# HGRN2 in a hybrid encoder: the 8-token base products of both heads of a pair in one run of half-array passes

## The chip, the cores and the metric

The kernel runs on one core of one Trainium2 chip. A core has five engines that work side by side, each through its own list of instructions in order: PE (TensorE, matrix products), DVE (VectorE, elementwise), ACT (ScalarE, elementwise and copies), POOL (GpSimd, elementwise) and SP (SyncE, which issues DMAs). An instruction waits, on its own engine, until the instructions it depends on have signalled. Products go to PSUM, a memory of eight banks of 128 x 512 fp32; everything else lives in SBUF. The metric is the device time of one execution in microseconds (us).

## The reference

A two-layer encoder on 512 tokens with 1024 channels, in fp32. Each layer feeds the same x through one input projection into three branches (HGRN2, a dilated sliding-window attention, a latent attention), gates and merges them, projects and normalizes. What the change touches is the HGRN2 branch, a gated linear recurrence run in both directions over 8 heads:

```python
def _gla_scan(q, k, v, log_f):
    '''S_t = diag(f_t) S_{t-1} + k_t v_t^T ; o_t = S_t^T q_t, chunkwise.'''
    ...
    def step(state, inp):
        qi, ki, vi, fi = inp
        b = jnp.cumsum(fi, axis=2)
        o_inter = jnp.einsum('bhtk,bhkv->bhtv', qi * jnp.exp(b), state)
        diff = b[:, :, :, None, :] - b[:, :, None, :, :]
        decay = jnp.where(causal, jnp.exp(jnp.where(causal, diff, 0.0)), 0.0)
        attn = jnp.einsum('bhtk,bhsk,bhtsk->bhts', qi, ki, decay)
        o = o_inter + jnp.einsum('bhts,bhsv->bhtv', attn, vi)
        ...
o_f = _gla_scan(q, k_f, v, lf_f)
o_b = flip(_gla_scan(flip(q), flip(k_b), flip(v), flip(lf_b)))
return (o_f + o_b).reshape(B, S, HG_HEADS * HG_DV)
```

## The kernel before, in words

**Layout.** Channels lie on the 128 partitions, the 512 tokens along the free dimension. An input projection of 128 channels (L300) is 24 PE passes of 128x128 weights against 512 tokens: three products of high and low parts of x and of the weights (`xh`, `xl`; `w_...h`, `w_...l`), eight passes each. The high part of a weight block is made by ACT (L274) and the low part by DVE or POOL (L275).

**HGRN2.** The eight heads are worked in four pairs. For a pair, `hgrn_gates` (L300, L677 to L689) projects `hq`, `hf` (two directions) for each head, 144 passes, and L689 clamps the forget gates `fr`. `hgrn_levels` then works up a tree: at level m = 1, 2, 4, 8, 16, 32, 64 blocks of m tokens are joined to blocks of 2m. Each level multiplies gates into queries (`qq`, L774), into keys (`kk`, L775) and gates into each other (`fr` or `f`, L778), all on DVE. The first product, `qq = q * fr`, is POOL's (L696).

- At m = 4 the **base products** are made: the scores inside blocks of 8 tokens, both directions. DVE takes the reciprocal of the gates (L706); the operands `hk` and `hq` are made half by ACT copies (L714) and half by POOL multiplications (L716), four each a head; sixteen products 64 rows wide go into a bank `hs` (L726, 32 records of 128x64 in the trace, since an fp32 product has two). ACT copies the bank to `hc` (L730), POOL cuts it to triangles `ha` and `hz` (L735), DVE adds them (L739).
- At m = 8 to 64 ACT copies the keys into `kc` (L745), sixteen **level products** a head follow (L757, bank `hs_8`, `hs_16` and so on), and DVE writes them into `ha` under a mask (L767). Only then may `qq` be multiplied on (L774), and only then can the products of the next level start.
- Then come key transposes `hkt` (L790) with their ACT copies (L792), state products `hst` (L801), the state chain `hS` on DVE (L810 to L818), and for the pair the outputs `ho` (L840).

Products 64 rows wide use half of PE's array; they are written as runs, between which PE does projections of the next pair.

**What joins a run.** `hgrn_levels` is a generator. A driver runs the two heads' generators in step; where they yield a list of instructions and a function, it calls both functions one after the other and lets the first product wait for both lists, so that both heads' products stand in one run. The level products and the states are yielded so. The base products are not: each head emits its own, with its own wait.

**What sets the order.** The engines' lists are not written by hand. A scheduler at build time places every recorded instruction by a cost model of its own and by program order, so a change in one place can reorder all engines around it. While a pair is in its tree, PE gets the passes of the next pair's gates and, for pairs 1 and 2, of `dv` (96 passes a block, L319), in pair 4 those of `dl`, `hgg` and others.

Of the kernel before, what the change touches and what calls it, by code (L numbers as in the profile page):

```python
# [45 lines left out]
HALVES = [(slice(64 * i, 64 * i + 64), slice(c + 64 * i, c + 64 * i + 64)) for c in range(0, S, 128) for i in range(2)]  # L46
# [144 lines left out]
def fap(ap, off, dims):  # L191

    return bass.AP(ap.tensor, ap.offset + off, [list(ap.ap[0])] + [list(d) for d in dims])
# [7 lines left out]
def tile_encoder(ctx: ExitStack, tc: tile.TileContext, x, xt, positions, blocks, wuq, wuh, par_in, brow, lbp,  # L201
                 ln_g, ln_b, consts, masks, out):
    nc = tc.nc
# [16 lines left out]
    def t2(name, dt=F32, tag="a2"):  # L220
        return t2p.tile([128, 512], dt, tag=tag, bufs=BUFS[tag], name=name)
# [7 lines left out]
    def at_bank(name):  # L229
        return ps_at.tile([128, 512], F32, tag="at", name=name)  # L230
# [4 lines left out]
    def after(first, *before):  # L235

        for b in before:
            tc.add_manual_dep(first.ins, b.ins.name, mybir.DependencyInfo(
                mybir.DependencyClass.Sync, mybir.DependencyReason.DATA), reason="together")
# [221 lines left out]
    def layer(l, x_src, need_next):  # L461
# [230 lines left out]
        def hgrn_levels(h, g, v):  # L692
# [4 lines left out]
            f2 = t2(f"f2{h}_{l}")  # L697
# [4 lines left out]
            while m < 128:  # L702
                if m == 4:
# [4 lines left out]
                    kds, qds, made = [], [], []  # L708
                    for d in range(2):
# [9 lines left out]
                                fap(rc, R * (1 - d) + scaled // m, [[2, R // 2], [0, m]]), ALU.mult))  # L719
                        kds.append(kd)  # L720
                        qds.append(qd)
                    sc, c = at_bank(f"hs{h}_{l}"), t2(f"hc{h}_{l}")
                    first = None
                    for d in range(2):
                        for n, (rows, at) in enumerate(HALVES):
                            mat = nc.tensor.matmul(sc[rows, 256 * d + 64 * (n // 2):256 * d + 64 * (n // 2) + 64],  # L726
                                                   kds[d][:, at], qds[d][:, at], start=True, stop=True)
                            first = first or mat
                    after(first, *made)
                    A.copy(c, sc)  # L730

                    for d, dst in ((0, a), (1, z)):
# [7 lines left out]
                elif m > 4:  # L740

                    if m < 64:
                        sc = at_bank(f"hs{h}_{m}_{l}")
                    kc = t2(f"kc{h}_{m}_{l}")
                    made = A.copy(fap(kc, 0, [[2 * m, R // 2], [m, 2], [1, m]]),  # L745
                                  fap(kk, 0, [[2 * m, R // 2], [S + m, 2], [1, m]]))
# [15 lines left out]
                    if m != 32:  # L762
                        n = [m in ms for ms in HG_MASKS].index(True)
                        for cols in [slice(0, 128)] if m == 64 else [slice(0, 64), slice(64, 128)]:
                            rows, wd = slice(0, 128) if m == 64 else cols, cols.stop - cols.start
# [21 lines left out]
            for d, blocks in ((0, (0, 1, 2)), (1, (1, 2, 3))):  # L787
# [4 lines left out]
                made = A.copy(kt_[:, :384], tr[:, :384])  # L792
# [23 lines left out]
            for j in (1, 0):  # L816
                c = 192 + 64 * j
# [48 lines left out]
        def dil_qk(hp):  # L866
            t = []
            for g in range(3):
                both = t4(f"dl{g}{hp}_{l}")
                for c0, sc_ in ((C_DQ[g], con[:, O_QS + 4 * g + hp:O_QS + 4 * g + hp + 1]), (C_DK[g], None)):  # L870
                    c = c0 + 128 * hp
                    ps = in_fm(c, f"dl{c}")
                    r = both[:, len(t) % 2]
                    o_ap, i_ap = r, ps
                    if g:
                        o_ap = r.rearrange("p (r i) -> p i r", r=4)
                        i_ap = ps.rearrange("p (i r) -> p i r", r=4)
                    if sc_ is None:
                        A.activation(o_ap, i_ap, AF.Identity, bias=pb(c))
                    else:  # L880
                        last = V.tensor_scalar(o_ap, i_ap, pb(c), sc_, ALU.add, ALU.mult)  # L881
                    t.append(r)
            return t, last
# [231 lines left out]
        for hp in range(4):  # L1115
            both = [hgrn_levels(h, G.pop(h), hv) for h in (2 * hp, 2 * hp + 1)]
            while True:
                parts = [next(g) for g in both]
                if parts[0] is None:
                    continue  # L1120
                if len(parts[0]) > 2:
                    break

                firsts = [go() for _, go in parts]
                after(firsts[0], *parts[0][0], *parts[1][0])
            os_.append(hgrn_pair(hp, parts, hv))
            if hp < 3:
                for h in (2 * hp + 2, 2 * hp + 3):
                    G[h] = hgrn_gates(h)
            if hp < 2:  # L1130
                vs.append(in_tm(C_DV[hp], f"dv{hp}", residues=hp > 0))
        hg = [silu_tile(C_HG + 128 * i, f"hgg{i}", False) for i in range(4)]
        qk, _ = dil_qk(0)
# [167 lines left out]
```

## Time and profile before

| | |
|---|---|
| median of three runs | 1773.09 us (1772.72 to 1774.57) |
| the profiled execution | 1771.63 us |
| its span, first to last instruction | 1769.9 us |
| PE busy | 1741.8 us, 98% of the span |
| DVE busy | 1064.2 us, 60% |
| ACT busy | 730.3 us, 41% |
| POOL busy | 573.8 us, 32% |
| mean granted PE clock | 0.996 of full speed |
| PE idle for DVE's `qq` (L774) ahead of level products | 4.3 us in 6 waits |
| base products | 8 heads in each of 2 layers, 32 records each |

A row of the timeline gives the start in us, the duration, the engine, the line, the operation, the tile written and the tiles read, the shape, how many instructions the row stands for, and in brackets the idle time before it with what ended it. The timeline leaves out the idle time of PE when two runs merely follow each other with a seam. PE's busy time counts a record at half clock as busy for twice as long, so "98% busy" holds slow stretches too; the windows' PEclk shows them.

### The profile page before, as it was taken

The numbers are of one execution on the slowest core, as the hardware profiler recorded it, in microseconds if no ns is written. First come the engines' busy times: TensorE is split into PE (matmuls) and PEld (weight loads), VectorE is DVE, ScalarE is ACT, GpSimd is POOL, SyncE is SP. The second block draws the span as 40 slices with busy tenths as digits, with TensorE's granted clock in tenths as the row PEclk, the third lists the DMA queues.
The fourth block names the chain that finished last, engine by engine and source line by source line (L and its number), as shares of the span: only waits on it lengthen the run. The fifth ranks groups of instructions, "written<-read, shape, count | busy, mean of one in ns | idle before, by whom it ended". The sixth has DMA issues, their size and how long they took to land. (4 is left out here: it accounts for less than half of the span.)

```text
span 1769.9 us, 26458 instructions
## 1 busy us (share of the span) xinstructions
PE 1741.8 (98%) x10616; PEld 1450.5 (82%) x10616; DVE 1064.2 (60%) x1912; ACT 730.3 (41%) x1273; POOL 573.8 (32%) x338
## 2 busy tenths in 40 slices
PE   9999999999999999999999999999999999999997
PEld 7778978988888888887888888888888888888876
DVE  8888777443232566756777778775333324666576
ACT  6445454242424353433254455442424254444330
POOL 0412244233333233333213212532433332433341
PEclk9999999999999999999999999999999999999999
DMA  5223222223222222332332222222223221324221
GB/s 194 84 66 102 73 73 89 73 72 96 79 77 84 70 75 79 113 111 72 119 114 90 84 78 74 89 78 78 72 72 98 82 83 48 99 67 151 72 86 69
DMA packets 77146, 154.15 MB, mean 87 GB/s; under 512 B 37728, under 2 KB 37856, under 8 KB 77024
## 3 DMA queue, kind: packets, MB, share of 16 engines
q1 hardware_dynamic: 77024, 152.47, 27.9%
q8 instruction: 83, 1.36, 0.3%
q14 instruction: 39, 0.32, 0.1%
HBM read 148.15 MB, written 4.29 MB: 86 GB/s over the span
## 5 line engine op out<-in xcount | busy, mean ns | idle before, releaser
L775 DVE TENSOR_TENSOR kk<-kk,fr 128x512 f32<-128x512 f32 x96 | 94.0, 999 | 30.0 <-ACT kc L745 18.9
L696 POOL TENSOR_TENSOR qq<-hq,fr 128x1024 f32<-128x1024 f32 x16 | 42.5, 2654 | 201.6 <-DVE fr L689 181.9
L774 DVE TENSOR_TENSOR qq<-qq,fr 128x512 f32<-128x512 f32 x96 | 75.3, 797 | 16.9 <-POOL qq L696 15.2
L1079 DVE TENSOR_SCALAR mg<-mg 128x512 f32<-128x512 f32 x32 | 53.2, 1669 | 49.0 <-ACT mg L1078 48.9
L898 DVE CUSTOM_DVE_ANT_0 zb<-dsb,con 128x256 f32<-128x256 f32 x64 | 23.3, 421 | 46.4 <-PE dsb L951 46.3
L767 DVE COPY_PREDICATED ha<-mask,hs 64x256 f32<-64x256 uint8 (+1 forms) x80 | 40.4, 505 | 16.7 <-PE hs L757 15.6
L275 POOL TENSOR_TENSOR wb_1l<-wb_1r,wb_1h 128x1024 fp32r<-128x1024 f32 x12 | 29.5, 2460 | 63.6 <-ACT wb_1h L274 42.5
L275 POOL TENSOR_TENSOR wb_0l<-wb_0r,wb_0h 128x1024 fp32r<-128x1024 f32 x12 | 29.5, 2461 | 63.4 <-ACT wb_0h L274 42.4
L881 DVE TENSOR_SCALAR dl<-dl,par,con 128x512 f32<-128x512 f32 x24 | 25.8, 1075 | 38.0 <-PE dl L300 37.9
L735 POOL TENSOR_SCALAR_AFFINE_SELECT ha<-hc 128x256 f32<-128x256 f32 x32 | 13.8, 456 | 105.0 <-ACT hc L730 97.3
L658 ACT COPY mpt<-mtr 128x128 f32<-128x128 f32 x64 | 17.0, 266 | 74.4 <-DVE mpt L658 74.4
L757 PEld LDWEIGHTS hs<-qq,kc 128*64 128x64 f32 x1024 | 33.1, 137 | 16.2 <-issue 8.4
L999 ACT ACTIVATE za<-za,dst 128x256 f32<-128x256 f32 x64 | 30.0, 470 | 33.2 <-DVE dst L993 33.2
L757 PE MATMUL hs<-qq,kc 128*64 128x64 f32 x1024 | 38.0, 225 | 4.3 <-DVE qq L774 4.3
L716 POOL TENSOR_TENSOR hk<-kk,f 128x256 f32<-128x256 f32 x32 | 24.8, 775 | 51.5 <-DVE fr L778 51.5
L792 ACT COPY hkt<-hkt 128x384 f32<-128x384 f32 x32 | 15.3, 480 | 59.9 <-PE hkt L790 59.6
L745 ACT COPY kc<-kk 128x512 f32<-128x512 f32 x64 | 37.5, 618 | 4.6 <-DVE kk L775 4.6
L658 DVE COPY mpt<-mtr 128x128 f32<-128x128 f32 x64 | 18.4, 288 | 32.7 <-PE mtr L655 22.3
L1079 DVE TENSOR_SCALAR mgc<-mgc 128x512 f32<-128x512 f32 x16 | 22.9, 1429 | 22.3 <-ACT mgc L1078 22.3
L1099 DVE TENSOR_TENSOR acc<-acc,mgc 128x512 f32<-128x512 f32 x16 | 32.2, 2049 | 0.0
L662 PE MATMUL mo<-mpt,mv 128*128 128x128 f32 (+1 forms) x192 | 31.9, 309 | 0.0
L1004 ACT ACTIVATE zb<-zb,dst 128x256 f32<-128x256 f32 x64 | 31.6, 495 | 0.0
(1509 smaller groups left out, 5400.8 us busy)
## 6 DMA issues: line engine op xcount, KB each, us to landing
wb_0r<-in_blocks_dram SPq DMA_DIRECT2D x12, 512.0 KB, 3.6
wb_1r<-in_blocks_dram SPq DMA_DIRECT2D x12, 512.0 KB, 3.6
w_0r<-in_blocks_dram SPq DMA_DIRECT2D x9, 512.0 KB, 3.4
w_1r<-in_blocks_dram SPq DMA_DIRECT2D x8, 512.0 KB, 3.6
w_2r<-in_blocks_dram SPq DMA_DIRECT2D x8, 512.0 KB, 3.5
w_3r<-in_blocks_dram SPq DMA_DIRECT2D x8, 512.0 KB, 3.6
wo_0r<-in_blocks_dram SPq DMA_DIRECT2D x8, 512.0 KB, 3.6
wo_1r<-in_blocks_dram SPq DMA_DIRECT2D x8, 512.0 KB, 3.5
```

Of the source, the lines that this page charges most:

```text
L275: (eng or nc.gpsimd).tensor_tensor(lo, raw, hi.bitcast(F32), ALU.subtract)
L658: (A.copy if kb % 2 else V.tensor_copy)(pts[kb][:, qs], tr[:, kb * 128:kb * 128 + 128])
L662: nc.tensor.matmul(o[:, cols], v[:, kb, h * 128:h * 128 + 128], pts[kb][:, cols], start=qt == 1 and kb == 0, stop=qt == NT - 1 and kb == N ...
L696: nc.gpsimd.tensor_tensor(qq, bcast(q, [[0, 2], [1, S]]), fr, ALU.mult)
L745: made = A.copy(fap(kc, 0, [[2 * m, R // 2], [m, 2], [1, m]]), fap(kk, 0, [[2 * m, R // 2], [S + m, 2], [1, m]]))
L757: mat = nc.tensor.matmul(sc[rows, to], kc[:, at], rhs, start=True, stop=True)
L767: ready = [V.copy_predicated(fap(a[rows], cols.start, [[128, NT], [1, wd]]), bcast(mk, [[0, NT], [1, wd]]), fap(sc[rows], cols.start, [[12 ...
L774: V.tensor_tensor(fap(qq, 0, dims), fap(qq, 0, dims), qf, ALU.mult)
L775: V.tensor_tensor(fap(kk, 0, dims), fap(kk, 0, dims), kf, ALU.mult)
L1004: A.activation(z, z, AF.Exp, bias=stat[:, 1, i, r:r + 1], scale=-1.0, accum_out=den[:, 1, i, r:r + 1])
L1079: V.tensor_scalar(g, g, 0.5, 0.5, ALU.mult, ALU.add)
L1099: V.tensor_tensor(acc[dt_], acc[dt_], g, ALU.add)
```

## The change

The base products become a function that the generator yields with the list of what they wait for, as the level products are. The driver therefore emits both heads' base products in one run, and the first of them waits for the `hk` and `hq` of both heads. What used to follow a head's own products (ACT's copy `hc`, POOL's triangles, DVE's addition) now follows in program order after both heads' products. The tile `hc` moves from the pool of tag `a2` to that of `f2`.

```diff
-                    sc, c = at_bank(f"hs{h}_{l}"), t2(f"hc{h}_{l}")
-                    first = None
-                    for d in range(2):
-                        for n, (rows, at) in enumerate(HALVES):
-                            mat = nc.tensor.matmul(sc[rows, 256 * d + 64 * (n // 2):256 * d + 64 * (n // 2) + 64],
-                                                   kds[d][:, at], qds[d][:, at], start=True, stop=True)
-                            first = first or mat
-                    after(first, *made)
+                    sc, c = at_bank(f"hs{h}_{l}"), t2(f"hc{h}_{l}", tag="f2")
+
+                    def base_products(sc=sc):
+                        first = None
+                        for d in range(2):
+                            for n, (rows, at) in enumerate(HALVES):
+                                mat = nc.tensor.matmul(sc[rows, 256 * d + 64 * (n // 2):256 * d + 64 * (n // 2) + 64],
+                                                       kds[d][:, at], qds[d][:, at], start=True, stop=True)
+                                first = first or mat
+                        return first
+
+                    yield made, base_products
                     A.copy(c, sc)
```

Behind the diff every line number is four higher (two at the base products). Each engine has the same number of instructions; their order is not the same.

PE in layer 0, first pair (heads 0 and 1; `hq_893` and `hf_929` are projections of the next pair, `hs_0_609` the base products of head 0, the other bank those of head 1), as a difference, before with - and after with +:

```order
-L726 MATMUL hs_0_609<-hq_0_598,hk_0_597 64x64 x8
-L726 MATMUL hs_0_609<-hq_0_604,hk_0_603 64x64 x8
+L728 MATMUL hs_0_609<-hq_0_598,hk_0_597 64x64 x8
+L728 MATMUL hs_0_609<-hq_0_604,hk_0_603 64x64 x8
+L728 MATMUL hs_0_626<-hq_0_615,hk_0_614 64x64 x8
+L728 MATMUL hs_0_626<-hq_0_621,hk_0_620 64x64 x8
 L300 MATMUL hq_893<-xh,w_256h 128x512 x8
 L300 MATMUL hq_893<-xl,w_256h 128x512 x8
 L300 MATMUL hq_893<-xh,w_256l 128x512 x8
```

Head 1's products stood 40 passes further on (`hs_0_651`, between two groups of `hf_929`); now they stand ahead of the first of those passes.

DVE at the same place, from head 1's reciprocal to the addition that empties the bank `hv_0`, after the change (before it, the rows `kk_0_313` and `qq_0_579` are not there: they stand behind all four `hv` additions):

```order
L706 RECIPROCAL f_0_581<-fr_0_312 128x256
L782 TENSOR_TENSOR fr_0_312<-fr_0_312 128x128
L275 TENSOR_TENSOR w_256l<-w_256r,w_256h 128x1024
...
L338 TENSOR_SCALAR r_w<-r_w 128x512
L779 TENSOR_TENSOR kk_0_313<-kk_0_313,fr_0_312 128x2x64x4
L373 SCALAR_TENSOR_TENSOR r_r<-r_n,r_r 128x512
L275 TENSOR_TENSOR w_1280l<-w_1280r,w_1280h 128x1024
L782 TENSOR_TENSOR fr_0_312<-fr_0_312 128x32
L778 TENSOR_TENSOR qq_0_579<-qq_0_579,fr_0_312 128x2x64x4
L342 TENSOR_TENSOR r_u<-r_u,r_w 128x512
L516 TENSOR_TENSOR hv_385<-hv_0_412,hvb_386 128x512
```

`kk_0_313` and `qq_0_579` overwrite what POOL's `hk` and `hq` of head 1 read, so they wait for POOL, and the addition waits behind them.

POOL in layer 0, third pair (heads 4 and 5), after the change:

```order
L716 TENSOR_TENSOR hk04_0_1910<-kk4_0_1579,f24_0_1891 128x64x4
L716 TENSOR_TENSOR hq04_0_1911<-qq4_0_1889,f24_0_1891 128x64x4
L716 TENSOR_TENSOR hk14_0_1916<-kk4_0_1579,f24_0_1891 128x64x4
L716 TENSOR_TENSOR hq14_0_1917<-qq4_0_1889,f24_0_1891 128x64x4
L716 TENSOR_TENSOR hk05_0_1927<-kk5_0_1686,f25_0_1894 128x64x4
L716 TENSOR_TENSOR hq05_0_1928<-qq5_0_1892,f25_0_1894 128x64x4
L716 TENSOR_TENSOR hk15_0_1933<-kk5_0_1686,f25_0_1894 128x64x4
L716 TENSOR_TENSOR hq15_0_1934<-qq5_0_1892,f25_0_1894 128x64x4
L739 AFFINE_SELECT ha4_0_1908<-hc4_0_1923 128x4x64 x2
```

Before, the triangles of head 4 (`ha4`, `hz4`) stood between `hq14` and `hk05`, that is, head 5's operands were made after head 4's base products had run.

DVE in the same pair, from the clamp of the next pair's gates to the multiplications that let the level products of m = 32 start; first before the change:

```order
L689 TENSOR_SCALAR fr6_0_2235<-fr6_0_2235 128x1024
L775 TENSOR_TENSOR kk5_0_1686<-kk5_0_1686,fr5_0_1685 128x2x4x64
L775 TENSOR_TENSOR kk6_0_2236<-kk6_0_2236,fr6_0_2235 128x2x256
L767 COPY_PREDICATED ha4_0_1908<-mask_91,hs4_16_0_2023 64x4x64 x2
L774 TENSOR_TENSOR qq4_0_1889<-qq4_0_1889,fr4_0_1578 128x2x16x16
L767 COPY_PREDICATED ha5_0_1950<-mask_91,hs5_16_0_2026 64x4x64 x2
L774 TENSOR_TENSOR qq5_0_1892<-qq5_0_1892,fr5_0_1685 128x2x16x16
```

and after:

```order
L771 COPY_PREDICATED ha4_0_1908<-mask_91,hs4_16_0_2023 64x4x64 x2
L778 TENSOR_TENSOR qq4_0_1889<-qq4_0_1889,fr4_0_1578 128x2x16x16
L771 COPY_PREDICATED ha5_0_1925<-mask_91,hs5_16_0_2026 64x4x64 x2
L778 TENSOR_TENSOR qq5_0_1892<-qq5_0_1892,fr5_0_1685 128x2x16x16
L275 TENSOR_TENSOR w0_2944l_2382<-w0_2944r_2379,w0_2944h_2381 128x1024
L689 TENSOR_SCALAR fr6_0_2235<-fr6_0_2235 128x1024
```

The clamp L689, which POOL's L696 waits for, stood ahead of the masked copies and multiplications of m = 16 and stands behind them now. The first pair of layer 0 shows the same move, from row 135 to row 141 of DVE's list with the copies of m = 16 at rows 141 and 136.

## The prediction

> **What bounds the kernel now.** I read the page's busy times first, then the waits of PE, then the timeline of PE at the HGRN2 stage, and last DVE's and POOL's timelines around each wait. The busy line of the page and the three largest waits of PE:
>
> ```profile
> PE 1741.8 (98%) x10616; PEld 1450.5 (82%) x10616; DVE 1064.2 (60%) x1912; ACT 730.3 (41%) x1273; POOL 573.8 (32%) x338
> ```
>
> ```profile
> PE mtr L655 <- DVE mp L652: 5.2, 4, 1.5
> PE hs L757 <- DVE qq L774: 4.3, 6, 1.0
> PE hq L300 <- ACT w_2304h L274: 3.3, 1, 3.3
> ```
>
> PE sets the time: whatever shortens the kernel either takes work or seams off PE, or takes away one of its idle spells. No PE instruction is removed here. The first wait lies in the latent attention, whose order does not change; the second and third lie in the stage that the change reorders. So three things can move: seams between runs, the 4.3 us ahead of the level products, and the 3.3 us in the first pair.
>
> **Seams.** PE in layer 0, pair 3, around a lone run of half-array products (L757, 32 records), and in pair 2 around base products that stand directly behind `ho`:
>
> ```profile
> 227.25 1.98 PE L300 MATMUL hq<-xl,w_896h 128*128 128x512 f32 x8
> 229.06 0.61 PE L300 MATMUL hq<-xh,w_896l 128*128 128x512 f32 x2
> 229.61 1.15 PE L757 MATMUL hs<-qq,kc 128*64 128x64 f32 x32
> 230.69 1.66 PE L300 MATMUL hq<-xh,w_896l 128*128 128x512 f32 x6
> 232.18 1.98 PE L300 MATMUL hf<-xh,w_1920h 128*128 128x512 f32 x8
> ```
>
> ```profile
> 136.47 0.39 PE L840 MATMUL ho<-qq,hS 128*64 128x128 f32 x4
> 136.68 1.10 PE L726 MATMUL hs<-hq,hk 128*64 128x64 f32 x32
> 137.71 1.66 PE L300 MATMUL hq<-xh,w_512h 128*128 128x512 f32 x6
> ```
>
> Eight passes take 229.06 - 227.25 = 1.81 us, 0.2265 each. Eight passes with a run of 32 among them take 232.18 - 229.06 = 3.12, so a lone run costs 1.31. A run joined to another costs 137.71 - 136.68 = 1.03. A seam saved is worth about 0.28. The words of the change promise one saved for each of the eight pairs, 2.2 us. The order says otherwise: in three of the four pairs of a layer head 1's base products already stood next to the previous pair's `ho`, as at 136.68, and afterwards `ho` stands alone. Runs of half-array products go from 58 to 56. Two seams at 0.28: **-0.5 us** (bounds -0.4 to -0.9; the last if transposes `hkt`, joined in five pairs, save a little too, which no row prices).
>
> **The waits for `qq`.** The six of that row are two in pair 1 of layer 0, and one each in pairs 3 and 4 of both layers. PE, pair 1, then pair 3, then pair 4 of layer 0:
>
> ```profile
> 102.42 0.69 PE L757 MATMUL hs<-qq,kc 128*64 128x64 f32 x16 [0.24 <-DVE qq L774]
> 104.06 0.69 PE L757 MATMUL hs<-qq,kc 128*64 128x64 f32 x16 [0.95 <-DVE qq L774]
> 104.68 0.55 PE L790 MATMUL hkt<-con,kk 128*128 128x128 f32 x3
> ...
> 236.61 0.69 PE L757 MATMUL hs<-qq,kc 128*64 128x64 f32 x16
> 238.26 0.69 PE L757 MATMUL hs<-qq,kc 128*64 128x64 f32 x16 [0.96 <-DVE qq L774]
> 238.88 0.55 PE L790 MATMUL hkt<-con,kk 128*128 128x128 f32 x3
> ...
> 299.80 0.69 PE L757 MATMUL hs<-qq,kc 128*64 128x64 f32 x16 [0.59 <-DVE qq L774]
> ```
>
> These are the products of m = 32: the run breaks in the middle, since head 2's `qq` is late. Pair 3 needs 238.88 - 236.61 = 2.27 us for a run that takes 230.69 - 229.61 = 1.08: it loses 1.19, of which the bracket shows 0.96. Pair 1 loses 2.26 - 1.08 + 0.24 = 1.42. DVE and POOL in pair 3 show what makes `qq` late:
>
> ```profile
> 230.16 3.50 DVE L775 TENSOR_TENSOR kk<-kk,fr 128x512 f32<-128x512 f32 x2
> 233.68 0.91 DVE L767 COPY_PREDICATED ha<-mask,hs 64x256 f32<-64x256 uint8 x2
> 234.60 1.87 DVE L774 TENSOR_TENSOR qq<-qq,fr 128x512 f32<-128x512 f32 x1
> 236.50 0.91 DVE L767 COPY_PREDICATED ha<-mask,hs 64x256 f32<-64x256 uint8 x2
> 237.42 1.29 DVE L774 TENSOR_TENSOR qq<-qq,fr 128x512 f32<-128x512 f32 x2
> ```
>
> ```profile
> 230.33 2.78 POOL L696 TENSOR_TENSOR qq<-hq,fr 128x1024 f32<-128x1024 f32 x1 [9.88 <-PE hs L757]
> ```
>
> Two multiplications that take 1.29 at 237.42 take 3.50 at 230.16, while POOL's L696 runs; one takes 1.87 at 234.60. The masked copies that should follow PE's products of m = 16 at 230.69 start at 233.68. Left alone, the chain is two copies (0.91), a `qq` (0.65), two copies, a `qq`: 3.1 us.
>
> In the new order POOL's L696 can't be there: DVE's clamp L689, for which it waits, stands behind the copies and `qq` of m = 16 in pairs 1 and 3. PE has 22 passes or more (4.98 us) between the products of m = 16 and 32, against 3.1 plus some signals, so a slack near 1.7 us. I take these three stalls as gone: 1.42 + 2 x 1.19 = **-3.8 us**. Bounds: if they all stay 0; more than -3.8 isn't there, except pair 4's 0.59 twice, which I leave, since POOL's weight splits still stand there. The cover of the moved L696 is the 20 passes (4.5 us) up to the products of m = 64, which need two `qq` (1.29) and may lose 3.50 - 1.29 = 2.2 to it: 3.5 of 4.5, so some 1 us is left.
>
> **The first pair of layer 0.** PE idles here for a bank that DVE empties by adding `hv` (the releaser that the wait names, a cast, ended with it by chance). PE, then windows of it (columns: window, length, busy and count of PE, PEld, DVE, ACT, POOL, then the granted clock), then the other engines:
>
> ```profile
> 61.52 1.15 PE L726 MATMUL hs<-hq,hk 128*64 128x64 f32 x32
> 65.99 3.75 PE L300 MATMUL hq<-xh,w_256h 128*128 128x512 f32 x8 [3.32 <-ACT w_2304h L274]
> 72.49 1.98 PE L300 MATMUL hq<-xh,w_256l 128*128 128x512 f32 x8
> ```
>
> ```profile
> 64.00:66.00 2.00, 0.01 (x1) 0.04 (x1) 2.00 (x5) 1.05 (x2) 0.00 (x0) 0.78 0.50 90
> 66.00:68.00 2.00, 2.00 (x5) 1.61 (x6) 2.00 (x5) 1.70 (x5) 1.45 (x4) 0.50 0.58 229
> ...
> 70.00:72.00 2.00, 2.00 (x6) 1.61 (x5) 2.00 (x3) 0.00 (x0) 2.00 (x2) 0.52 0.13 16
> 72.00:74.00 2.00, 2.00 (x10) 1.65 (x9) 1.97 (x4) 1.06 (x1) 0.52 (x1) 1.00 0.71 246
> ```
>
> ```profile
> 58.65 1.74 DVE L706 RECIPROCAL f<-fr 128x256 f32<-128x256 f32 x1
> ...
> 65.17 0.68 DVE L516 TENSOR_TENSOR hv<-hv,hvb 128x512 f32<-128x512 f32 x1
> ```
>
> ```profile
> 66.55 0.80 POOL L735 TENSOR_SCALAR_AFFINE_SELECT ha<-hc 128x256 f32<-128x256 f32 x2 [9.91 <-ACT hc L730]
> ...
> 68.05 1.09 POOL L716 TENSOR_TENSOR hk<-kk,f 128x256 f32<-128x256 f32 x1
> ...
> 71.41 1.11 POOL L716 TENSOR_TENSOR hq<-qq,f 128x256 f32<-128x256 f32 x1
> ```
>
> The idle spell halves the clock: 0.78 over 64 to 66 means that it fell at about 65.1, and it is back at 72.0. Sixteen passes from 65.99 to 72.49 take 6.50 instead of 3.62: 2.9 us lost beside the 3.32 of idling.
>
> Afterwards PE waits at 61.5 for head 2's operands. Its reciprocal ends at 60.39 and POOL is idle then; four products take 4.47 as at 68.05, or 4 x 0.68 = 2.7 left alone, so they end between 63.1 and 64.9. The run of both heads (2.1 us) ends near 66.1. Ahead of the `hv` addition DVE now has two multiplications more (0.65 each), the first with a wait of 0 to 1.0 for POOL's third product: the addition ends 1.3 to 2.3 later, and `hq` starts so much later. I take 1.9, start 67.9. Against it, head 1's own run (1.31) no longer stands 40 passes on. And the slow stretch: I keep its ends, 65.1 to 72.0, so that 4.1 us of projection fall into it instead of 6.0, 0.9 less lost. Sum 1.9 - 1.3 - 0.9 = **-0.3 us**; bounds +1.0 (2.3 later, as much lost to the clock as before) and -2.4 (1.9 later, no slow stretch).
>
> **Sum.** -0.5 - 3.8 - 0.3 = -4.6 us. The profiled execution's 1771.63 would be 1767.0. It lay 1.5 below the median of the runs; from 1773.09 it is **1768.5 us**. What can't be told from no change is about 0.2%, 3.5 us, so 1769.5 is the border of faster.
>
> **Rivals.** *The clock never falls* in the first pair: the idle time is then in two spells, 2.5 us (61.5 to 64) and 1.8 (66.1 to 67.9). For it: the clock fell 2.5 us into a spell of 3.32, and the spells of 1.5 at `mtr` left it at full speed. Against: together they are longer than the old one. That is -2.4 instead of -0.3: 1766.4. The Trainium skill, "TensorE: Matmul & The Clock Gate", section "What's actually happening", has the clock halve after an idle window of about 3.4 us, windows that run freely; no spell would be so long here, which gives this rival's time. But this trace's spell of 3.32 wasn't either, and its clock fell, so the trace does not bear the figure out to the letter.
>
> *The stall only moves.* L696 with its 2.78 us lands between m = 32 and m = 64, or on the operands of the next pair, and costs there what it cost before; the change is then two seams. Speaking for it: the margin of 1 us, and PE at 98%, where DVE's 60% is mostly in this stage. -0.5 - 0.3: 1772.3.
>
> *Head 2's operands are late.* PE, in order, now stands ahead of the base run until POOL has made eight products instead of four, and all projections stand behind that run. In pair 2 head 1's last is done at 131.98, and PE gets there at 136.68:
>
> ```profile
> 50.90 4.47 POOL L716 TENSOR_TENSOR hq<-qq,f 128x256 f32<-128x256 f32 x1
> ...
> 131.26 0.72 POOL L716 TENSOR_TENSOR hq<-qq,f 128x256 f32<-128x256 f32 x1
> ```
>
> Slack 4.7; four more at 0.68 leave 2.0. A single one that takes 4.47, as at 50.90, makes it 1.8 late. In six pairs (2 to 4 of both layers) 10.8: 1779.3; from 1.3 us each on it outweighs all gains by 3.5. Against it: DVE's list has head 2's reciprocal well ahead of the base run in these pairs, with some 3 to 6 us by my count. The Trainium skill, "SBUF — State Buffer", section "SBUF: two separate sides", makes this likelier: a DVE instruction with two SBUF inputs and a POOL one that reads SBUF shut each other out for a whole instruction. The stretched rows of both engines here fit it.
>
> **Chances.** Forecast 0.50 (own range 1766.5 to 1771, of it 0.34 beyond 0.2% and 0.16 within); clock never falls 0.14; stall only moves 0.20; operands late 0.16. Faster 0.34 + 0.14 = 0.48, same 0.16 + 0.20 = 0.36, slower 0.16. The range reaches down to 1764.5 (clock and all stalls, pair 4's too: -0.9 - 5.0 - 2.4 is -8.3) and up to 1775.5, which leaves out most of the last rival.
>
> **What would show it.** Right: the wait of `hs` for `qq` falls from 4.3 to about 1.2 us, with pair 4 alone left; no DVE multiplication of 1.8 us between m = 16 and 32; in the first pair `hq` starts near 67.9, and 72 to 74 is at full clock. Wrong: a wait of base products (L728) on POOL's or ACT's `hk` and `hq` in pairs 2 to 4, new waits at m = 8 or m = 64, or `hq` after 68.5 with the clock still at half past 72.

## The result, and the profile after

| | before | after |
|---|---|---|
| median | 1771.89 us | 1781.88 us (1780.96 to 1784.9) |
| ratio | 1 | 1.0058, 95% interval 1.0045 to 1.0071 |
| the profiled execution | 1771.63 us | 1784.9 us |

The changed kernel is slower by 0.58%, about 10 us, where 4.6 us less had been forecast; the upper end of the forecast's range was 1775.5. The profiled execution of the changed kernel lies 3 us above its median, and it has a wait of 1.6 us in the dilated attention (`do`) that the kernel before has not. Waits for `do` of 1.5 to 5.1 us stand in every run below except the one with the first pair alone joined, also in the one where no pair is joined; what brings them is not shown. So the reading below goes by the HGRN2 stage alone.

The waits of PE in the changed kernel:

```profile
PE hs L728 <- POOL hq L716: 7.0, 3, 2.8
PE hs L761 <- DVE qq L778: 5.3, 2, 2.7
PE mtr L655 <- DVE mp L652: 5.2, 4, 1.5
PE hs L761 <- ACT w_6144h L274: 2.3, 2, 1.2
PE do L1023 <- ACT dta31p L1039: 1.6, 1, 1.6
...
PE hq L300 <- DVE hv L516: 1.1, 1, 1.1
```

Of the waits in the HGRN2 stage, those of the base products are for POOL's `hq`: once in the first pair of layer 0 and once in pair 4 of each layer. The level products of m = 16 wait, in pair 4 of each layer, twice (the one that is put down to a cast also ends with DVE's `qq`, which is done at 287.43, as the rows below show). The old waits at m = 32 of pairs 1 and 3 are gone. Where the lag grows is read from two kinds of pass that both kernels have, the first gates that PE does in pair 2's tree and the latent compression of both layers; before:

```profile
137.71 1.66 PE L300 MATMUL hq<-xh,w_512h 128*128 128x512 f32 x6
...
L300 PE MATMUL ckv<-xh,w_9600h x16: 389/389/393, 588.5 to 1465.9; 128*128 128x512 f32 x16
```

and after:

```profile
139.32 2.11 PE L300 MATMUL hq<-xh,w_512h 128*128 128x512 f32 x8
...
L300 PE MATMUL ckv<-xh,w_9600h x16: 389/389/393, 594.2 to 1476.6; 128*128 128x512 f32 x16
```

After the first pair the changed kernel is 1.6 us late, of which 0.2 was there before the stage began and 1.0 is only that the base products of pair 2's second head are already done. Behind layer 0's HGRN2 it is 5.7 late, behind layer 1's 10.7. So the first pair costs some 0.4, layer 0's other pairs cost about 5, and so do the four of layer 1. PE in layer 0, pair 4, of the changed kernel:

```profile
269.88 2.09 PE L728 MATMUL hs<-hq,hk 128*64 128x64 f32 x64 [2.07 <-POOL hq L716]
...
287.57 0.69 PE L761 MATMUL hs<-qq,kc 128*64 128x64 f32 x16 [1.14 <-ACT w_6144h L274]
290.93 1.12 PE L761 MATMUL hs<-qq,kc 128*64 128x64 f32 x16 [2.67 <-DVE qq L778]
291.98 3.36 PE L300 MATMUL dl<-xl,w_4608h 128*128 128x512 f32 x7
295.13 2.38 PE L300 MATMUL dl<-xh,w_4608l 128*128 128x512 f32 x8
297.35 1.75 PE L300 MATMUL dl<-xh,w_5632h 128*128 128x512 f32 x7
```

PE waits 2.07 us ahead of the base run, then 1.14 and 2.67 around the products of m = 16, and behind them the passes run slow: 15 passes from 291.98 to 297.35 take 5.4 us instead of 3.4. DVE and POOL over the same stretch show why the operands, and later `qq`, come late:

```profile
249.32 2.65 DVE L778 TENSOR_TENSOR qq<-qq,f 128x512 f32<-128x512 f32 x1
251.89 0.68 DVE L779 TENSOR_TENSOR kk<-kk,f 128x512 f32<-128x512 f32 x1
...
260.32 2.88 DVE L779 TENSOR_TENSOR kk<-kk,f 128x512 f32<-128x512 f32 x1
...
265.46 1.74 DVE L706 RECIPROCAL f<-fr 128x256 f32<-128x256 f32 x1
...
270.37 2.86 DVE L779 TENSOR_TENSOR kk<-kk,fr 128x512 f32<-128x512 f32 x1
273.15 2.90 DVE L778 TENSOR_TENSOR qq<-qq,fr 128x512 f32<-128x512 f32 x1
...
279.58 2.65 DVE L779 TENSOR_TENSOR kk<-kk,fr 128x512 f32<-128x512 f32 x1
...
286.74 0.69 DVE L778 TENSOR_TENSOR qq<-qq,fr 128x512 f32<-128x512 f32 x1
...
289.01 1.77 DVE L778 TENSOR_TENSOR qq<-qq,fr 128x512 f32<-128x512 f32 x1
```

```profile
249.02 2.40 POOL L275 TENSOR_TENSOR w_3840l<-w_3840r,w_3840h 128x1024 fp32r<-128x1024 f32 x1 [4.80 <-issue]
...
259.81 2.84 POOL L275 TENSOR_TENSOR w_3968l<-w_3968r,w_3968h 128x1024 fp32r<-128x1024 f32 x1
267.27 0.68 POOL L716 TENSOR_TENSOR hk<-kk,f 128x256 f32<-128x256 f32 x1 [4.62 <-DVE f L706]
...
269.16 0.67 POOL L716 TENSOR_TENSOR hq<-qq,f 128x256 f32<-128x256 f32 x1
...
287.58 2.66 POOL L275 TENSOR_TENSOR w_6144l<-w_6144r,w_6144h 128x1024 fp32r<-128x1024 f32 x1 [5.89 <-ACT w_6144h L274]
```

The multiplication at 249.32 that takes 0.68 when alone (the row behind it) ends 0.55 us after POOL's split `w_3840l` (the subtraction of L275 that makes the low part of a weight block) ends at 251.42: it was held for the whole of it. The same happens at 260.32 beside `w_3968l`, and at 289.01 beside `w_6144l`. The second head's reciprocal ends at 267.20, POOL is idle for 4.62 us waiting for it, its four products end at 269.83, and PE, which got there at 267.81, starts at 269.88. The rows at 270.37, 273.15 and 279.58 stand beside the next three splits and end 0.54 to 0.56 after them. They lose some 6 us together, so that DVE comes to the masked copies of m = 8 at 285.82, though PE had made those products by 281.2, and `qq` for m = 16 follows from there.

Windows of PE in that pair, after (length, busy and count of PE, PEld, DVE, ACT, POOL, then the granted clock):

```profile
286.00:288.00 2.00, 0.86 (x16) 0.46 (x17) 1.97 (x4) 1.50 (x2) 0.42 (x1) 1.00 0.00 0
288.00:290.00 2.00, 0.26 (x9) 0.12 (x5) 1.91 (x4) 0.62 (x1) 2.00 (x1) 0.78 0.00 0
290.00:292.00 2.00, 1.07 (x17) 0.99 (x17) 1.98 (x3) 0.00 (x0) 0.23 (x1) 0.50 0.44 68
...
294.00:296.00 2.00, 2.00 (x7) 1.53 (x6) 1.89 (x4) 0.58 (x1) 0.00 (x0) 0.51 0.00 0
```

Behind the waits at m = 16 the clock is halved too, which in the profile of before happened, while PE had work, only in the first pair. Per layer, pair 4 thus pays 2.07 + 1.14 + 2.67 in waits and some 2.0 in slow passes, 7.9 in all, against 0.59 before.

### The profile page after: what moved, and what is told of

The parts are those of the page before. It is cut to its first block, busy times and chain, and to the rows that moved or that the text cites. A ratio compares the mean times of both kernels' runs of the same rounds, so it can differ in the third digit from the quotient of the medians.

```text
span 1782.7 us, 26468 instructions
## 1 busy us (share of the span) xinstructions
PE 1745.0 (98%) x10616; PEld 1453.1 (82%) x10616; DVE 1086.5 (61%) x1912; ACT 736.8 (41%) x1273; POOL 582.8 (33%) x338
## 4 chain that ended last, share of the span: by engine, by line
PE 86%; DVE 6%; issue 2%; POOL 2%; ACT 1%; DMA 1%; SPq 0%; DVEq 0%; ACTq 0%; POOLq 0%
PE mg L300 16%; PE dl L300 14%; PE hf L300 8%; PE dv L319 8%; PE br L1093 6%; PE hq L300 4%; PE dg L300 2%; PE wo L1254 2%; PE cq L300 2%; PE hs L761 2%; PE st L500 2%; PE do L1023 2%; PE mo L662 1%; PE ckv L300 1%; PE hv L319 1%
## 5 line engine op out<-in xcount | busy, mean ns | idle before, releaser
L696 POOL TENSOR_TENSOR qq<-hq,fr 128x1024 f32<-128x1024 f32 x16 | 41.9, 2616 | 271.8 <-DVE fr L689 271.8
L778 DVE TENSOR_TENSOR qq<-qq,fr 128x512 f32<-128x512 f32 x96 | 88.2, 926 | 8.5 <-PE hs L761 7.7
L779 DVE TENSOR_TENSOR kk<-kk,fr 128x512 f32<-128x512 f32 x96 | 86.5, 914 | 1.9 <-POOL hk L716 1.2
L275 POOL TENSOR_TENSOR wb_0l<-wb_0r,wb_0h 128x1024 fp32r<-128x1024 f32 x12 | 29.6, 2463 | 62.4 <-ACT wb_0h L274 41.4
L275 POOL TENSOR_TENSOR wb_1l<-wb_1r,wb_1h 128x1024 fp32r<-128x1024 f32 x12 | 29.6, 2464 | 61.9 <-ACT wb_1h L274 35.7
L716 POOL TENSOR_TENSOR hk<-kk,f 128x256 f32<-128x256 f32 x32 | 29.5, 922 | 50.6 <-DVE fr L782 34.4
L782 DVE TENSOR_TENSOR fr<-fr 128x128 f32<-128x128 f32 (+4 forms) x80 | 32.8, 422 | 0.7
L662 PEld LDWEIGHTS mo<-mpt,mv 128*128 128x128 f32 x192 | 28.8, 190 | 3.1
```

The source lines that it names most:

```text
L275: (eng or nc.gpsimd).tensor_tensor(lo, raw, hi.bitcast(F32), ALU.subtract)
L662: nc.tensor.matmul(o[:, cols], v[:, kb, h * 128:h * 128 + 128], pts[kb][:, cols], start=qt == 1 and kb == 0, stop=qt == NT - 1 and kb == N ...
L696: nc.gpsimd.tensor_tensor(qq, bcast(q, [[0, 2], [1, S]]), fr, ALU.mult)
L778: V.tensor_tensor(fap(qq, 0, dims), fap(qq, 0, dims), qf, ALU.mult)
L779: V.tensor_tensor(fap(kk, 0, dims), fap(kk, 0, dims), kf, ALU.mult)
```

## The experiments

The theory after the result, **A**: the joined run itself does what was forecast, and the whole loss sits in pair 4, where DVE's multiplications and POOL's weight splits shut each other out and the new order asks for the results earlier. Its rivals were that the order is worse in all pairs (B), that pair 4 is late only because of what the other pairs do (C, and later H), that the move of `hc` to the other pool is at fault (E), that DVE is simply too full (D), and that POOL's queue, not the exclusion, is late (A2). All ratios below are against the kernel before on the same chip, with 95% intervals.

### The joined run in some pairs, with the pool move

```diff
-                    yield made, base_products
+                    if h < 6:                     # second run: if h >= 6
+                        yield made, base_products
+                    else:
+                        after(base_products(), *made)
```

> The joined run in pairs 1 to 3 of both layers; in pair 4 each head's base products with a wait of their own, as before. hc stays in the other pool. Theory A (the loss sits in pair 4, where POOL's weight splits and DVE's multiplications shut each other out): the waits of pair 4 of 2.06, 1.15 and 2.67 us a layer go, 1781.9 falls by some 9.5 to about 1772.5. Theory B (the loss is spread over all pairs, since DVE's list is worse everywhere): at most half of it goes, 1777 or more.

> The joined run in pair 4 of both layers alone, hc in the other pool everywhere. In the built order the run stands directly behind ho, 63 passes after the states hst. Theory A: pair 4 loses by itself, a wait ahead of the run or, since only 24 passes lie between it and the products of m = 8, there and at m = 16; 1776 to 1782. Theory C (pair 4 is late only because pairs 1 to 3 are reordered, which brings its base run nearer to its gates): 1771 to 1774.

Measured: pairs 1 to 3, 1.0037 (1.0022 to 1.0052), about 6.5 us; pair 4 alone, 1.0076 (1.0061 to 1.0091), 13.5 us, more than the whole change. The first is a number that B had given (1777 or more), the second lies above what either theory gave. Neither number speaks for or against a theory, since `hc` stayed in its new pool. The waits of PE in the run with pairs 1 to 3 show a wait that neither kernel has:

```profile
PE dl L300 <- DVE hgg0s L529: 5.9, 2, 2.9
```

In pair 4 `dl`'s first pass waits for a bank that ACT and DVE must empty into `hgg0s`, a tile of the pool into which `hc` was moved. The pool had to be looked at by itself.

### The pool move alone, and the change without it

```diff
-                    sc, c = at_bank(f"hs{h}_{l}"), t2(f"hc{h}_{l}")
+                    sc, c = at_bank(f"hs{h}_{l}"), t2(f"hc{h}_{l}", tag="f2")
```

> Only hc is moved to the other pool of tiles, no joined run. The order then has head 2's base products of pair 4 two passes behind head 1's. Theory A: what matters is that head 2's base products are brought forward in pair 4, by whatever means: slower by 2 to 8 us, 1774 to 1780. Theory B or C: the pool does nothing, 1771.9 within 1.

> The joined run in all pairs, with hc left in its old pool of 16 tiles. In the pool of 8 hc stands in one ring with the tiles into which ACT reads the hgg banks, so that in pair 4 the drain of hgg0 waits for hc, hc for the base products, and dl for the bank: in the changed kernel that drain starts at 272.49, before the change at 253.84. Theory E (the pool ring is a part of the loss): drain of hgg0 near 254 again, base run of pair 4 a few passes later, 1774 to 1778. Theory A alone (only POOL's splits): nothing changes, 1780 to 1783. If the pool were the whole loss, 1768.5 as predicted.

Measured: the kernel before with the pool move alone 1.0148 (1.0132 to 1.0165), 26 us slower, where no theory had given more than 8; the change without the pool move 1.0074 (1.0059 to 1.0090), not different from the change with it. The first has two waits of 6.95 us for POOL's `hq` and two of 2.06 for `hgg0s`:

```profile
285.61 1.97 PE L726 MATMUL hs<-hq,hk 128*64 128x64 f32 x32 [6.95 <-POOL hq L716]
289.64 3.78 PE L300 MATMUL dl<-xh,w_4096h 128*128 128x512 f32 x8 [2.06 <-DVE hgg0s L529]
```

So the pool of eight ties `hgg`'s drain to `hc`, and without a joined run that is dear. With the joined run in all pairs it does nothing that can be told: theory E falls for the change as it stands. With pair 4 alone joined the move is dear again: 1.0076 with it, 1.0014 without (below). The runs that follow leave `hc` where it was, unless they say otherwise.

### POOL's splits taken away

```diff
-        hgrn = key[0] == "tm" or key[0] == "fm" and key[1] < C_HG
+        hgrn = key[0] == "tm" or key[0] == "fm" and (key[1] < C_HG or key[1] in (3584, 3712, 3840, 3968,
+                                                     4096, 4608, 5632, 6144, 7168, 7680))
```

> The changed kernel, with the low parts of the ten weight blocks (hgg and the first dl) that are used during pair 4 made by DVE instead of POOL, in both layers. Theory A: POOL no longer runs 2.4 to 2.9 us instructions in pair 4 that shut DVE out; the wait of base products for POOL's hq in pair 4 (2.06 a layer) and the two at m = 16 (1.15 and 2.67) go, and the time falls to 1771 to 1774, although DVE has 12 us more to do in a layer. Theory D (DVE is simply too full there, 91% busy from 245 to 270 us): it stays or gets worse, 1781 or more.

> Control: the kernel before, with the ten low parts of pair 4 made by DVE instead of POOL. Theory A: before the change the splits hid, except 0.59 us a layer at m = 32 of pair 4, so 0 to -1.5: 1770.6 to 1772.4. Theory F (the splits are worth 10 us to any version, so that their move says nothing about the change): 1762 to 1766.

Measured: the changed kernel so edited 0.9999 (0.9990 to 1.0009), ten microseconds less than without the edit; its waits hold none in pair 4 for POOL or for `qq`, but one of 1.32 a layer for `hgg0s`, since `hc` is in the pool of eight here. The kernel before with the same edit 0.9985 (0.9976 to 0.9994), 2.7 us less. So the move returns 7 us more to the changed kernel than to the old one, and theory D, that DVE has no room, falls: DVE took the ten splits, and pair 4 ran without those waits. That the splits are worth 10 us to any version (F) falls too. But the edit also moved the built order (90 passes instead of 72 between the gates of pair 4 and its base run), so it does not show the exclusion by itself.

For that the ten splits were replaced by fills, which write the tile and read nothing, with their low parts left out of the result; first one fill each, then three, which take as long as a split:

```diff
+        if any(name.endswith(f"_{c}") for c in (3584, 3712, 3840, 3968, 4096, 4608, 5632, 6144, 7168, 7680)):
+            nc.gpsimd.memset(lo.bitcast(F32), 0.0)     # second run: three of them
+        else:
             (eng or nc.gpsimd).tensor_tensor(lo, raw, hi.bitcast(F32), ALU.subtract)
```

> The changed kernel in which POOL fills the ten low parts of pair 4 with zeros instead of subtracting (the low parts of hgg's and the first dl's weights are left out of the result). PE's order is the same row for row. POOL still has a 128x1024 instruction at each of these places, but it reads nothing from SBUF. Theory A1 (POOL's reading shuts DVE's two-input instructions out): the DVE multiplications of 2.6 to 2.9 us in pair 4 fall to 0.7, the waits of 2.06, 1.15 and 2.67 a layer go, 8 to 11 us less than the changed kernel. Theory A2 (POOL's own queue makes hk, hq and the triangles late): most of the waits stay, at most 4 us less.

> As the run in which POOL only writes, but with three fills in a row in place of each of the ten low parts (left out of the result), so that POOL is occupied as long as by a split (3 x 0.95 = 2.85 us against 2.40 to 2.90) and still reads nothing. PE's base run of pair 4 stands in the same place, 72 passes behind the pair's gates. Theory A1 (DVE is shut out while POOL reads): DVE keeps its 0.7 us instructions, at most half a microsecond of waits in pair 4, 1768 to 1770 where before is 1773. Theory A2 (POOL's time in its own queue is what delays hk, hq and the triangles): the wait of base products for hq of about 2 us and the one at m = 16 come back, 1776 or more.

Measured: 0.9971 (0.9960 to 0.9982), and with three fills 0.9984 (0.9974 to 0.9994). The first is 15 us less than the changed kernel, where A1 had given 8 to 11: that was the waits alone, and with the slow passes behind them, 2 x 7.9, the trace gives as much. POOL and DVE with three fills, at the place where the split held `qq` for 2.65 us:

```profile
249.26 2.98 POOL L277 MEMSET w_3840l<- 128x1024 f32 x3 [4.23 <-PE hf L304]
```

```profile
249.64 0.69 DVE L782 TENSOR_TENSOR qq<-qq,f 128x512 f32<-128x512 f32 x1
250.24 0.69 DVE L783 TENSOR_TENSOR kk<-kk,f 128x512 f32<-128x512 f32 x1
...
251.57 1.23 DVE L693 TENSOR_SCALAR fr<-fr 128x1024 f32<-128x1024 f32 x1
```

POOL is occupied from 249.26 to 252.24, and DVE's two-input multiplications run in 0.69 beside it. Beside the later fills they take 0.67 to 0.70 as well, the second `qq` for m = 16 (at 283.78) among them. Pair 4 has no wait in either run: PE starts its base run at once in the same place, 72 passes behind the gates. A2 falls, A1 holds: it is the reading that shuts DVE out. (The run with three fills has a wait of 1.7 us at m = 32 of the first pair that the other has not; it is a part of the difference between the two.) The Trainium skill states this lock in "SBUF — State Buffer", section "SBUF: two separate sides": a DVE instruction with two inputs in SBUF and a GpSimd one that reads SBUF exclude each other for a whole instruction; the trace agrees, with 2.65 us beside the split and 0.69 beside the fills.

With the splits not reading, the changed kernel is 0.29% faster than before, 5.1 us (3.2 to 7.1), and with three fills 2.8 (1.1 to 4.6). That is near the 4.6 forecast for the change as it stands, but it is not the change's own share: the fills were not put into the kernel before, where they could have taken away pair 4's 0.59 of each layer as well.

### Which pairs, without the pool move

```diff
-                    yield made, base_products
+                    if <pairs>:      # pairs 2, 3 and layer 1's pair 1 | first pair of layer 0 | pair 3 | pair 4
+                        yield made, base_products
+                    else:
+                        after(base_products(), *made)
```

> The joined run in pairs 2 and 3 of both layers and pair 1 of layer 1 alone, hc in its old pool; the first pair of layer 0 and both pairs 4 keep their own waits. This is the part in which the stall at m = 32 of pair 3 (1.19 us a layer) should go, with a seam or so. Theory: 1772.1 less 2.4 to 3.5, 1769 to 1770. Theory B (the new order costs everywhere): 1774 or more.

> The joined run in the first pair of layer 0 alone, hc in its old pool; all other pairs in the order of before. Theory: hq starts 3.4 us later than before the change, in a slow clock, head 1's run (1.31) moves ahead and the stall at m = 32 (1.42) goes: 0 to 2 us slower. As the prediction had it (-0.3 - 1.4): 1.7 us faster.

> The joined run in pair 3 of both layers alone, hc in its old pool. Theory H (joining in pair 3 brings its tree forward and so pair 4's base products, which then fall among POOL's splits): pair 3's stall of 1.19 goes, but pair 4 waits at m = 16 for some 6 us a layer, 7 to 10 us slower. Theory A in its first form (only pair 4's own joined run costs): 2.4 us faster.

> The joined run in pair 4 of both layers alone, hc in its old pool. In the built order the run stands directly behind ho, 66 passes after hst, with 28 passes to m = 8 and 27 to m = 16. Theory A in its first form: waits ahead of the run or at m = 8 and 16, 4 to 10 us slower. Theory H alone (it is all pair 3's doing): within 1.5 us of before.

Measured: middle pairs 1.0062 (1.0042 to 1.0082); first pair 1.0007 (0.9998 to 1.0017); pair 3 alone 1.0080 (1.0063 to 1.0098); pair 4 alone 1.0014 (1.0004 to 1.0023). Pair 3 alone was to cost 7 to 10 us by theory H, and pair 4 alone, 2.4 us slower, lies between what H (up to 1.5) and A in its first form (4 to 10) gave. The surprise is that joining in pair 3 costs 14 us, although pair 3 itself runs better: its wait at m = 32 is gone, and the loss is in pair 4, whose own products wait head by head as before. PE there, with pair 3 alone joined:

```profile
288.20 0.91 PE L764 MATMUL hs<-qq,kc 128*64 128x64 f32 x16 [2.24 <-DVE qq L781]
292.62 1.12 PE L764 MATMUL hs<-qq,kc 128*64 128x64 f32 x16 [3.51 <-DVE qq L781]
```

DVE and POOL between the two, once more a split (beside earlier ones three rows, at 261.07, 274.77 and 279.79, had taken 2.21, 2.22 and 2.88):

```profile
287.97 2.84 DVE L782 TENSOR_TENSOR kk<-kk,fr 128x512 f32<-128x512 f32 x1
```

```profile
287.46 2.80 POOL L275 TENSOR_TENSOR w_6144l<-w_6144r,w_6144h 128x1024 fp32r<-128x1024 f32 x1 [5.34 <-ACT w_6144h L274]
```

What the order gives explains it. Counted are the projection passes that PE does between the last gate of pair 4 and the pair's products; the chain of multiplications on DVE that must be done in that time is the same in all. The rows of pair 4, of pair 3, of pairs 2 and 3 and the first of all pairs have `hc` in its old pool, the last three in the new one:

| joined run in | passes to the second head's base products | passes to m = 16 | waits of pair 4, layer 0, at these products | ratio |
|---|---|---|---|---|
| none (before) | 133 | 187 | none (0.59 at m = 32) | 1 |
| pair 4 | 96 | 151 | 1.43 | 1.0014 |
| pair 3 | 83 | 136 | 2.24 + 3.51 | 1.0080 |
| pairs 2, 3 (and layer 1's pair 1) | 83 | 136 | 2.24 + 3.73 | 1.0062 |
| all, `hc` in its old pool | 75 | 129 | 1.94 + 0.81 + 2.07 | 1.0074 |
| all (the change) | 72 | 129 | 2.07 + 1.14 + 2.67 | 1.0058 |
| all, ten splits on DVE | 90 | 144 | none (1.32 for `hgg0s`) | 0.9999 |
| all, POOL only writes (one fill) | 72 | 129 | none | 0.9971 |

A joined run takes the 40 passes between the two heads' base products out of a pair's tree. Behind pairs 1 and 2 the 96 passes of `dv` make up for it: base products stay 96 passes or more behind the gates. Behind pair 3 there is no `dv`, and everything of pair 4 moves forward by some 50 passes, 11 us, into the time of POOL's splits. The row of the change and the last have the same order on PE, so it is not the nearness alone that makes the waits, but nearness and the reading splits together. The parts don't add up, since each moves pair 4 by itself; and the run with pairs 1 to 3 and the pool move can't be set beside these rows, since in its pair 4 PE waits 2.93 for `hgg0s` ahead of m = 16. Theory B falls: pairs 1 to 3 of the changed kernel have no wait behind their base products, and the loss is in pair 4. Theory A in its first form falls too: it is not pair 4's own joined run that costs most, but the place to which pair 3's brings it. H holds, and C before it, in their sense though not in their numbers.

### What could be kept

> The joined run everywhere but in the first pair of layer 0, hc in its old pool, the ten low parts of pair 4 made by DVE. All three sources of loss are taken away: pair 4's waits, the pool ring, and the first pair with its slow clock (about 3 us). Theory: the predicted gain of pair 3 and of pair 4's m = 32 is left, 1772.1 - 2.4 - 1.2 - 0.5, about 1768. If it stays at 1772 or above, a further loss is not named yet.

> A version that could be kept: the joined run in all pairs, hc in its old pool, and only those five of the ten low parts on DVE that stand in the way in pair 4 (two of hgg's, three of dl's). The built order has 94 passes from the gates of pair 4 to its base run, 154 to m = 16, instead of 72 and 129. Theory: pair 4 without waits, or with less than 1 us a layer; pairs 1 and 3 without their old stalls; the first pair 1.5 us slower: 1773 - 3.8 - 0.6 + 1.5, near 1770, 0.9984. If pair 4 still waits: 1773 or more.

```diff
+        hgrn = ... or key[1] in (<the ten>)                          # first run
+                    if l or h >= 2: yield made, base_products        # first run
+        hgrn = ... or key[1] in (3840, 3968, 4096, 4608, 6144)       # second run, all pairs joined
```

Measured: 0.9984 (0.9975 to 0.9993) and 0.9990 (0.9981 to 1.0000). Both have no wait of pair 4 above 0.4 us. The first had been put about 4 us below the kernel before and lies 2.9 below it; in its first pair, left as it was, PE waits 0.73, 1.55, 0.66 and 0.94 at m = 16 and 32, where the kernel before has 0.24 and 0.95. Neither beats the kernel before with its ten splits on DVE (0.9985): where DVE takes the splits, pair 3's old stall is gone in the old order as well, and the joined run has nothing left to gain there. That control is the simplest version that beats both kernels, by 0.15% on the one and some 0.7% on the other.

## Why the prediction was right or wrong

**The waits at m = 32, -3.8 us: right.** The chain of the order (L689 behind the copies of m = 16, so L696 later) did what was said: the stretched multiplications of pair 3 now lie behind the products of m = 32, and pairs 1 and 3 have no wait there. In layer 0's pair 3 both runs, m = 32 and m = 64, are whole, and DVE's stretched row lies between them:

```profile
228.43 1.15 PE L761 MATMUL hs<-qq,kc 128*64 128x64 f32 x32
...
234.57 1.15 PE L761 MATMUL hs<-qq,kc 128*64 128x64 f32 x32
```

```profile
229.56 3.49 DVE L778 TENSOR_TENSOR qq<-qq,fr 128x512 f32<-128x512 f32 x2
```

The margin at m = 64, put at 1 us, held. The saving is read from the waits that are gone; no run shows it alone, since each that joins pair 3 moves pair 4 with it.

**Seams, -0.5 us: not shown apart.** No run isolates them. The count (58 to 56, not a seam for each pair) held. The kernels with the splits on DVE, joined and not, come out alike, but they differ in more than seams, so they give no bound.

**The first pair, -0.3 us: mis-sized.** PE and the windows after:

```profile
64.62 3.68 PE L728 MATMUL hs<-hq,hk 128*64 128x64 f32 x64 [2.84 <-POOL hq L716]
69.36 3.78 PE L300 MATMUL hq<-xh,w_256h 128*128 128x512 f32 x8 [1.06 <-DVE hv L516]
...
75.32 1.98 PE L300 MATMUL hq<-xh,w_256l 128*128 128x512 f32 x8
```

```profile
62.00:64.00 2.00, 0.00 (x0) 0.00 (x0) 2.00 (x4) 0.00 (x0) 2.00 (x4) 0.96 0.53 176
...
72.00:74.00 2.00, 2.00 (x6) 1.53 (x5) 2.00 (x4) 0.00 (x0) 0.00 (x0) 0.50 0.05 16
74.00:76.00 2.00, 2.00 (x10) 1.63 (x9) 2.00 (x5) 1.06 (x2) 0.00 (x0) 0.98 0.80 246
```

```profile
61.73 0.88 DVE L337 TENSOR_SCALAR r_w<-r_u 128x512 f32<-128x512 f32 x1
62.53 0.88 DVE L338 TENSOR_SCALAR r_n<-r_n 128x512 f32<-128x512 f32 x1
63.34 0.68 DVE L782 TENSOR_TENSOR fr<-fr 128x64 f32<-128x64 f32 x1
63.95 0.90 DVE L338 TENSOR_SCALAR r_w<-r_w 128x512 f32<-128x512 f32 x1
...
68.63 0.68 DVE L516 TENSOR_TENSOR hv<-hv,hvb 128x512 f32<-128x512 f32 x1
```

Operands at 64.6, within the bounds (63.1 to 64.9); `hq` at 69.36, behind the latest that had been allowed (68.3), since the `hv` addition came at 68.63 (65.17 before). The sum had two multiplications of 0.65 and a wait of up to 1.0 ahead of it. The multiplications cost 1.2, but four small instructions of DVE were stretched too while POOL worked, the one at 61.73 to 0.88 from 0.41 before, and cost 1.9 more together. And the slow stretch did not keep its ends: it lasted from 63.8 to 74.1, so the third block of eight starts 2.83 later than before; less the second head's run (1.31), 1.5 instead of -0.3. With the stall of that pair gone, the pair as a whole was to give 1.7 and the run with the first pair alone gave 1.0007 (0.9998 to 1.0017), 1.2 us slower. The rival of a clock that never falls was wrong in this trace. (Its sum of no slow stretch, 1.9 - 1.3 - 2.9, is -2.3, not -2.4; nothing hangs on it.)

**Pair 4: the step that failed.** It stands in the rival of late operands: "Against it: DVE's list has head 2's reciprocal well ahead of the base run in these pairs, with some 3 to 6 us by my count." For pairs 2 and 3 that held. In pair 4 the reciprocal ended at 267.20, 0.6 us before PE came, and four products of POOL still had to follow. The prediction does not show how it counted; with DVE's multiplications at their length alone, as beside the fills, the reciprocal ends at 263.91, 3.9 before PE came in the changed kernel, which fits its 3 to 6. On that reading what it left out are POOL's splits of 2.4 to 2.9 us beside them, though it had shown exactly such a pair of rows for pair 3 and priced it there. From the first `hS` copy of pair 3 to the second head's reciprocal of pair 4 DVE took 247.11 to 267.20, 20.1 us; with POOL only writing it took 247.43 to 263.91 in the run with three fills, 16.5. The 3.6 us between are more than the 2.07 that PE waited. The rival had the wait and named the lock, and its price is near (1.8 late; measured 2.07), but that is luck: the 1.8 came from one POOL multiplication stretched to 4.47, where POOL's four took 0.66 to 0.68 each and it was DVE that was late. It spread the price over six pairs where it came in two, and it stopped at the base products: the 3.8 us of waits at m = 16 in each layer and the slow clock behind them were in no case. "Pair 4's 0.59 twice, which I leave, since POOL's weight splits still stand there" was the other place where the splits had been seen and not followed: they stood there, and the products of m = 16 had come 58 passes nearer to the pair's gates. In the terms of the sum, -3.8 for the old stalls, 1.5 for the first pair and 2 x 7.3 for pair 4 make 12.3; by the lag behind layer 1's HGRN2 it is 10.5 (10.7 less the 0.2 from before the stage), and the rest is not told apart.

**What was said to show it wrong** did, but for m = 16, which was not among the signs: a wait of base products on POOL's `hq`, though in pair 4 alone, and `hq` after 68.5 with the clock at half past 72.

## What to carry to other kernels

When a change shortens one stage's chain, ask what the engines behind it are brought up against: count, in the built order, the passes between a producer's end and its consumer, before and after, for every stage, also for those whose code is untouched. Price a chain on DVE with POOL's instructions running beside it, not by its uncontended rows, wherever the trace shows one such stretched row. And an edit that also moves a tile to another ring of buffers is two edits: time each alone before reading the pairs.

## What the runs showed of the hardware

- **DVE and POOL.** A two-input DVE multiplication of 0.68 us took 2.65 beside a POOL subtraction of 2.40 and 0.69 beside fills of 2.98. Instructions with a single input were not free either: in the first pair one of 0.41 took 0.88 while POOL multiplied, and one did wait for fills: the clamp at 251.57 took 1.23 instead of 0.69 and ended 0.56 us after the fills' end at 252.24.
- **The granted clock.** By the windows the slow stretch of the first pair lasted from 65.1 to 71.9 before the change and from 63.8 to 74.1 after it, that of pair 4 from 289.1 to 296.0: 6.8, 10.2 and 6.8 us. The length of a wait does not decide alone whether the clock falls. Waits of 2.84, and of 1.14 and 2.67 with a half run between, went with a fall, while with the pool move alone a wait of 2.81 ahead of 66.69 left the clock at 1.00 from 60 to 74. Single waits of 1.5 at `mtr` left it at full speed before the change; with pair 4 alone joined it was at half from 104.8 to 108.2, 3.4 us, behind waits of only 0.71 and 0.94. The Trainium skill, "TensorE: Matmul & The Clock Gate", section "What's actually happening", has the clock fall after an idle window and gives freely running windows of 3413 ns: the four lengths are two, three, two and one of them, so the traces agree there. They do not agree that a whole window must be idle: at 65.1 before the change PE had been idle for 2.4 us.
